# An encoder block on one core: modulation columns, output weights' sums and gate transposes placed earlier, pooling of one group placed later, and the end of each scan placed in the next head's scan

## The chip, the cores and the metric

The kernel runs on one core of a Trainium2 chip. The metric is the device time of one execution in microseconds (us); the kernel before takes 2042.19 us (median of three runs, 2037.84 to 2043.9).

The engines named below are TensorE (PE, with PEld for its weight loads), VectorE (DVE), ScalarE (ACT), GpSimd (POOL) and SyncE (SP). SP issues nearly all DMA transfers, in one queue.

## The reference, cut to what matters

One layer, 2048 tokens, model width 1024: modulation from `c`, a token mixer with two halves (a bidirectional mLSTM of 4 heads and a pooling of 4 channel groups), then a squared-ReLU MLP.

```
mod = silu(c) @ w_ada + b_ada              # 6 x 1024: sh1, sc1, gt1, sh2, sc2, gt2
h   = rmsnorm(x) * (1 + sc1) + sh1
q, k, v, o, gates, u = split(h @ w_in)     # 4 heads of 128; u: 4 groups of 128
hm  = scan_forward(q, k, v, gates) + scan_backward(...)     # in chunks of 128 tokens
y_a = sigmoid(o) * headnorm(hm) * g_head
y_b = ((mean of u over a window 2, 4, 8, 16) - u) @ w_pool * pool_scale
x   = x + gt1 * (concat(y_a, y_b) @ w_out)
h   = rmsnorm(x) * (1 + sc2) + sh2
x   = x + gt2 * (relu(h @ w_ff1)^2 @ w_ff2)
out = rmsnorm(x)
```

## The kernel before, in words

**Stages.** TensorE goes through the program in this order: a first part of the modulation (columns 0 to 15 of 48, each a 128x1024 piece of `w_ada`) and the projection of v and the gates (16 blocks of 128 tokens, `vg_mm` and `vg_out`); the pool stage (`for g in (3, 2, 1, 0)`, each with four blocks of 512 tokens); the q and k projection of head 0; four scans, each over 16 chunks, beside which the next head's projection (the last scan's: the o projection) is issued; then the output projection and the MLP, which the change does not touch.

**A projection block.** `col_mm(ci, b, w)` multiplies column group `ci` with token block `b`: 8 k-steps of three matmuls each, high weight by high activation (L404), high by low (L405) and low by high (L406). The split weights come from `col_weights(ci)`: a load of 512 KB into a buffer `wr`, a cast on ScalarE to `wh`, and on VectorE `wl = wr - wh` (L396). The pool stage uses column group 12+g for pool group g, so 15, 14, 13, 12, and then 4 for the q and k projection. The weights of the next one are asked for at block 1 of the group ahead of it.

**One group of the pool stage.** ScalarE copies each block's sum from PSUM into `u` (L440). When all four blocks are there, VectorE sums over the window by doubling (`s`, L447 and L451: one addition for window 2, four for window 16), mends the edges and subtracts `u` (L456); the result `yd` is stored. Then comes a fold: a piece of the output weights is loaded (`wor`), scaled on VectorE, multiplied with `w_pool` on TensorE (`wof`, two matmuls), copied and stored (`wod`). Then the modulation columns that `MODS[g]` lists are summed, each by `mod_col(j)`: a load of 512 KB (`ada`) and one multiply-and-sum on VectorE (L117).

**Gates.** `gate_rows` is a generator which the pool stage steps once per block. It transposes the gates (`gT`), makes log-sigmoids and running sums on VectorE and ScalarE, transposes the last elements (`gL`, L335), and later `gM`, `gC` and `gD`.

**Sums of the output weights.** `out_sums` makes the seven 512-wide combinations of `w_out * gt1` that the output projection wants: for each of four k two loads of 512 KB, two multiplications (L674), four subtractions (L682) and seven stores of 256 KB. It is stepped from the loop over the scans.

**Buffers.** `wr`, `ada`, `wor` and `os` (the tiles of `out_sums`) share three buffers (`raw`); evacuations share three (`evt`). Projection blocks share two PSUM buffers, folds two.

**Order.** The code's order is a starting point: a scheduler sets the order of each engine's instructions within what dependencies allow, save those that `keep_in_program_order` pins. Each engine then runs its instructions in the order that it was given.

Of the kernel before, what the change touches and what calls it, by code (L numbers as in the profile page):

```python
# [30 lines left out]
MODS = (range(16, 20), range(20, 28), range(28, 38), range(38, 48))  # L31
# [4 lines left out]
def block_kernel(ctx, tc, x, x_t, cb, w_ada, b_ada, g_mix, g_ffn, g_head, p_scale, w_col, w_vg,  # L36
# [96 lines left out]
    with tc.tile_pool(name="pv", bufs=1) as pv, tc.tile_pool(name="psV", bufs=2, space=PSUM) as psV:  # L133
# [156 lines left out]
        for b in range(NB):  # L290
            if b + 1 < NB:
                dg, xk = later_block(b + 1)
            for j in range(4):
# [6 lines left out]
                vg_out(4 * b + j)  # L300

# [8 lines left out]
    def gate_rows(pg):  # L310
# [22 lines left out]
        yield  # L333
        ps = tp("gL")
        pe.transpose(ps[0:1, 0:P], lasts[:, 0:1], ident)  # L335
# [16 lines left out]
        pe.transpose(ps[:, 0:1], rows[:, 3, :], ident[0:1, 0:1])  # L352
# [21 lines left out]
        yield  # L374
        ps = tp("gC")
        pe.transpose(ps[:, 0:P], v, ident)
# [36 lines left out]


    with tc.tile_pool(name="pu", bufs=2) as pu, tc.tile_pool(name="psU", bufs=2, space=PSUM) as psU:
# [7 lines left out]
        w = col_weights(15)  # L423
        for g in (3, 2, 1, 0):
            win = WIN[g]
            hw = win // 2
            u = pu.tile([P, T + 16], F32, tag="u", name=f"u{g}")
            gp.memset(u[:, 0:8], 0.0)
            gp.memset(u[:, T + 8:T + 16], 0.0)
            for b in range(NB):  # L430
# [10 lines left out]
                if b == 1:  # L441
                    wn = col_weights(11 + g if g else 4)
            w = wn

            s = pu.tile([P, T + 16], F32, tag="s", name=f"s{g}", bufs=1)
            n = T + 15
            ve.tensor_tensor(s[:, 0:n], u[:, 0:n], u[:, 1:n + 1], ALU.add)  # L447
            d = 2
            while d < win:
                n -= d  # L450
                ve.tensor_tensor(s[:, 0:n], s[:, 0:n], s[:, d:n + d], ALU.add)  # L451
                d *= 2
            s = s[:, 8 - hw:8 - hw + T]
            ve.tensor_tensor(s[:, 0:8], s[:, 0:8], edgec[:, 16 * g:16 * g + 8], ALU.mult)
            ve.tensor_tensor(s[:, T - 8:T], s[:, T - 8:T], edgec[:, 16 * g + 8:16 * g + 16], ALU.mult)
            ve.scalar_tensor_tensor(s, s, 1.0 / win, u[:, 8:8 + T], ALU.mult, ALU.subtract)  # L456
            for b in range(NB):
                dma(y_d[b][:, 4 + g, :], s[:, 512 * b:512 * b + 512])

            wr = raw(f"wor{g}")  # L460
            dma(wr, w_o[4 + g])
            ve.tensor_scalar(wr, wr, pscale[:, g:g + 1], None, ALU.mult)
            for n in range(2):
                ps = psU.tile([P, 512], F32, tag="y", name=f"wof{g}_{n}")
# [12 lines left out]
    with tc.tile_pool(name="ps_", bufs=2) as sp, tc.tile_pool(name="psS", bufs=1, space=PSUM) as psS:  # L477

        def qk_proj(h, C):
# [68 lines left out]
            for _ in p:  # L548
                yield

        def scan(h, Cb):
            X = {}

            def s0(c):
# [146 lines left out]
        for h in range(H):  # L701
# [6 lines left out]
            for _ in scan(h, Cb):  # L708
# [3 lines left out]
                if h > 0 and n % 4 == 0:  # L712
                    next(osum, None)
# [557 lines left out]
```

## Time and profile before

| | us |
|---|---|
| median of 3 runs (lowest, highest) | 2042.19 (2037.84, 2043.9) |
| profiled execution: device time, span in the trace | 2039.14, 2037.1 |
| TensorE busy | 1987.5 (98%) |
| VectorE busy | 1356.5 (67%) |
| ScalarE busy | 918.3 (45%) |
| GpSimd busy | 129.7 (6%) |
| data moved by DMA | 452.87 MB |

The device time of the profiled execution is 2 us above the span of its trace, and 3 us under the median of the timed runs. TensorE's granted clock is 0.997 of full speed over the execution. The stages of the trace, by TensorE's matmuls: the projection of v and the gates until 134.3 us, the pool stage until 239, q and k of head 0 until 290.6, the four scans from 290.6, 377.5, 459.7 and 534.5, and from 640 us the output projection and the MLP.

### The profile page before, as it was taken

To read this page: it belongs to the slowest core of one execution; us is meant where nothing else is said; L and a number is where in the kernel's file an instruction comes from. 1 tells how busy PE (TensorE), PEld (TensorE's weight loads), DVE (VectorE), ACT (ScalarE), POOL (GpSimd) and SP (SyncE) were. 2 spreads that over 40 slices of the span, in tenths; PEclk is the share of its full clock that TensorE was granted. 3 is DMA by queue.
4 is the path that set the end of the run, shared out by engine and by line. 5 is a ranking of instruction groups with operands and counts; after the bars stand their busy time and mean duration, and the time that the engine had idled before them with its cause. 6 is when DMAs were issued, how large, how long until landed. Compare 5 with 4: busy or idle time off the path is not lost.

```text
span 2037.1 us, 27780 instructions
## 1 busy us (share of the span) xinstructions
PE 1987.5 (98%) x9591; PEld 1658.5 (81%) x9591; DVE 1356.5 (67%) x2456; ACT 918.3 (45%) x1704; POOL 129.7 (6%) x353
## 2 busy tenths in 40 slices
PE   7999999989999999999999999999999999999998
PEld 6997777778887888888888888888888888888886
DVE  6638636676646777555666766666877667768876
ACT  4721223333335668755556655556324224324432
POOL 1100012222210111000000000000000000000011
PEclk9999999999999999999999999999999999999999
DMA  8736867787548799765666766766887657648553
GB/s 339 237 108 209 285 205 220 253 254 226 180 131 271 236 270 315 209 196 182 224 203 224 228 226 215 226 206 225 280 268 257 225 156 262 224 158 275 187 165 132
DMA packets 298574, 452.87 MB, mean 222 GB/s; under 512 B 23569, under 2 KB 163137, under 8 KB 298306
## 3 DMA queue, kind: packets, MB, share of 16 engines
q1 hardware_dynamic: 228546, 413.35, 62.3%
q10 hardware_dynamic: 69888, 37.76, 6.1%
q8 instruction: 75, 1.23, 0.2%
q14 instruction: 65, 0.53, 0.1%
HBM read 290.40 MB, written 160.62 MB: 221 GB/s over the span
## 4 chain that ended last, share of the span: by engine, by line
PE 84%; DMA 7%; DVE 4%; issue 1%; ACT 1%; POOL 1%; SPq 1%; POOLq 0%; DVEq 0%; ACTq 0%
PE c L405 4%; PE c L404 4%; PE c L406 4%; DMA ua<-uad 1%; DMA ada<-in_w_ada 1%; DVE ada L117 1%; DMA wotd<-os 1%; DMA rob<-wotd 1%; DMA vraw<-in_w_v 1%; PE f000x L845 1%; PE o11x L845 1%; PE o10x L845 1%; PE o13x L845 1%; PE o03x L845 1%; PE o12x L845 1%
## 5 line engine op out<-in xcount | busy, mean ns | idle before, releaser
L404 PE MATMUL c<-Hh,wh 128*128 128x512 f32 x512 | 211.0, 412 | 0.0
L405 PE MATMUL c<-Hl,wh 128*128 128x512 f32 x512 | 203.4, 397 | 0.0
L406 PE MATMUL c<-Hh,wl 128*128 128x512 f32 x512 | 202.8, 396 | 0.5 <-DVE wl L396 0.5
L406 PEld LDWEIGHTS c<-Hh,wl 128*128 128x128 f32 x512 | 96.6, 189 | 20.5 <-DVE wl L396 0.9
L404 PEld LDWEIGHTS c<-Hh,wh 128*128 128x128 f32 x512 | 97.0, 189 | 17.3 <-issue 1.0
L405 PEld LDWEIGHTS c<-Hl,wh 128*128 128x128 f32 x512 | 97.1, 190 | 16.8 <-issue 0.7
L117 DVE SCALAR_TENSOR_TENSOR ada<-ada,c_bc 128x1024 f32<-128x1024 f32 x48 | 58.1, 1221 | 22.4 <-DMA ada<-in_w_ada 22.3
L581 ACT ACTIVATE ua<-ua,vcol 128x128 f32<-128x128 f32 x64 | 25.7, 401 | 103.2 <-POOL ua L577 103.1
L780 ACT CAST wb<-rwb 128x1024 fp32r<-128x1024 f32 x56 | 58.7, 1051 | 26.0 <-DMA rwb<-twd 25.8
L961 POOL TENSOR_TENSOR g300ss<-g300ss 128x1 f32<-128x1 f32 x2 | 0.9, 451 | 1079.9 <-ACT g300j L957 1079.9
L783 DVE TENSOR_TENSOR wb<-rwb,wb 128x1024 fp32r<-128x1024 f32 x56 | 68.3, 1219 | 0.8 <-ACT wb L780 0.7
L622 ACT ACTIVATE jk<-hm 128x128 bf16<-128x128 f32 x64 | 19.6, 307 | 83.0 <-DVE hm L620 82.3
L586 DVE TENSOR_TENSOR ua<-ua,q 128x256 f32<-128x256 f32 x64 | 26.4, 425 | 37.5 <-DMA ua<-uad 26.8
L577 POOL TENSOR_SCALAR_AFFINE_SELECT ua<-ua 128x128 f32<-128x128 f32 x64 | 26.6, 416 | 270.7 <-DMA ua<-uad 135.4
L625 DVE TENSOR_TENSOR hm<-hm,hss 128x256 f32<-128x256 f32 x32 | 14.7, 458 | 38.9 <-POOL hss L129 38.9
L255 PE MATMUL vgp<-vgh,Hh 128*128 128x272 f32 x128 | 38.2, 301 | 2.3 <-ACT Hh L208 2.3
L440 ACT COPY u<-c 128x512 f32<-128x512 f32 x16 | 9.4, 585 | 63.7 <-PE c L406 59.4
L783 DVE TENSOR_TENSOR ob<-rob,ob 128x1024 fp32r<-128x1024 f32 x14 | 17.1, 1224 | 30.5 <-ACT ob L780 29.9
L256 PE MATMUL v2p<-v2h,Hh 128*128 128x256 f32 x128 | 36.2, 286 | 1.1 <-ACT v2h L236 1.1
L257 PE MATMUL vgp<-vgl,Hh 128*128 128x272 f32 x128 | 37.2, 292 | 0.0
L259 PE MATMUL vgp<-vgh,Hl 128*128 128x272 f32 x128 | 37.0, 294 | 0.0
L585 DVE TENSOR_TENSOR ua<-ua,S 128x256 f32<-128x256 f32 x64 | 26.5, 413 | 14.9 <-PE S L584 14.7
(4048 smaller groups left out, 6071.3 us busy)
## 6 DMA issues: line engine op xcount, KB each, us to landing
rwb<-twd SPq DMA_DIRECT2D x56, 512.0 KB, 6.1
ada<-in_w_ada SPq DMA_DIRECT2D x48, 512.0 KB, 5.2
ua<-uad SPq DMA_DIRECT2D x64, 256.0 KB, 4.1
j<-in_w SPq DMA_DIRECT2D x32, 512.0 KB, 5.4
twd<-t SPq DMA_DIRECT2D x64, 256.0 KB, 3.0
twd<-j SPq DMA_DIRECT2D x48, 256.0 KB, 2.8
wr<-in_w_col SPq DMA_DIRECT2D x16, 512.0 KB, 4.9
q<-qkd SPq DMA_DIRECT2D x32, 256.0 KB, 3.6
```

The lines of the kernel that those rows point to most:

```text
L117: ve.scalar_tensor_tensor(w, w, 1.0, c_bc, ALU.mult, ALU.mult, accum_out=mod[:, j:j + 1])
L255: pe.matmul(pa[:, :VG], hh, vgh[k], start=st, stop=False)
L256: pe.matmul(pb[:, :256], hh, v2h[k], start=st, stop=False)
L257: pe.matmul(pa[:, :VG], hh, vgl[k], start=False, stop=False)
L259: pe.matmul(pa[:, :VG], hl, vgh[k], start=False, stop=en)
L404: pe.matmul(ps, hh[:, k], Hh[b][:, k], start=k == 0, stop=False)
L405: pe.matmul(ps, hh[:, k], Hl[b][:, k], start=False, stop=False)
L406: pe.matmul(ps, hl[:, k], Hh[b][:, k], start=False, stop=k == KT - 1)
L577: gp.affine_select(W[:, 0], W[:, 0], pattern=[[1, P]], compare_op=ALU.is_ge, fill=NEG, base=0, channel_multiplier=-1)
L780: sc.copy(dst, src)
L783: ve.tensor_tensor(dst, src, asf(hi), ALU.subtract)
L845: pe.matmul(ps, a[:, k], b[:, k], start=start and k == 0 and n == 0, stop=k == 3 and n == 2, skip_group_check=not start)
```

## The change

1. Of the modulation's columns, 18 (16 to 33) are summed during blocks 8 to 13 of the projection of v and the gates (`VMODS`). The pool stage keeps 34 to 47, in another division (`MODS`).
2. `out_sums` becomes a function without steps that is called for k = 3, 2, 1, 0 at four places of the pool stage (`OSUMS`); `gt1` is made ahead of the stage. The scans no longer step it.
3. The gate transposes `gL`, `gM` and `gC` are pinned, and `gL` and `gC` come a block later.
4. The pooling of a group becomes the function `pooled`. That of group 3 is called, pinned, at the first block of group 2. Folds 3 and 2 stand behind group 3, folds 1 and 0 behind group 2 (`FOLDS`).
5. A scan's loop is one step shorter; its last pair of chunks is finished (`s3`, the transposes `hT`) at the start of the next head's scan.

```diff
-MODS = (range(16, 20), range(20, 28), range(28, 38), range(38, 48))
+VMODS = {i: range(16 + 3 * (i - 8), 19 + 3 * (i - 8)) for i in range(8, 14)}
+MODS = ((), range(44, 48), range(38, 44), range(34, 38))
+FOLDS = ((), (), (1, 0), (3, 2))
+OSUMS = {(2, 2): 3, (1, 0): 2, (1, 2): 1, (0, 0): 0}
...
                 vg_out(4 * b + j)
+                for n in VMODS.get(4 * b + j, ()):
+                    mod_col(n)
...
         yield
+        yield
         ps = tp("gL")
-        pe.transpose(ps[0:1, 0:P], lasts[:, 0:1], ident)
+        tc.keep_in_program_order(pe.transpose(ps[0:1, 0:P], lasts[:, 0:1], ident))
...
+    def out_sums(k, gt1):
+        rows = [raw(f"os{h}_{k}") for h in range(2)]
+        for h, src in enumerate((w_o[k], wo_d[k])):
+            dma(rows[h], src)
+        for h in range(2):
+            ve.tensor_tensor(rows[h], rows[h], gt1, ALU.mult)
+        b11, b12, b21, b22 = [r[:, 512 * n:512 * n + 512] for r in rows for n in range(2)]
+        for place, b in ((0, b11), (1, b21), (5, b22)):
+            dma(wot_d[place, :, k], b)
+        for place, dst, x_, y_ in ((3, b11, b12, b11), (4, b12, b22, b12), (2, b22, b22, b11),
+                                   (6, b21, b21, b22)):
+            ve.tensor_tensor(dst, x_, y_, ALU.subtract)
+            dma(wot_d[place, :, k], dst)
...
+        def pooled(g, u, pinned):
...
+            ins = ve.tensor_tensor(s[:, 0:n], u[:, 0:n], u[:, 1:n + 1], ALU.add)
+            if pinned:
+                tc.keep_in_program_order(ins)
...
                 if b == 1:
                     wn = col_weights(11 + g if g else 4)
+                if (g, b) in OSUMS:
+                    out_sums(OSUMS[g, b], gt1)
+                if (g, b) == (2, 0):
+                    pooled(3, u3, True)
             w = wn
...
+            if g == 3:
+                u3 = u
+            else:
+                pooled(g, u, False)
+            for f in FOLDS[g]:
+                wr = raw(f"wor{f}")
...
             for j in MODS[g]:
                 mod_col(j)
...
+            if ends:
+                ends.pop()()
-            for c in range(NT + 2):
+            for c in range(NT + 1):
...
+            if h + 1 < H:
+                ends.append(lambda: s3(NT - 1))
+            else:
+                s3(NT - 1)
...
-                if h > 0 and n % 4 == 0:
-                    next(osum, None)
```

What this does to the order of the engines' instructions is shown at three places. A number behind an underscore is that of the tile; `wl12` are the low weights of column group 12, `u1` and `s1` belong to pool group 1, and `os0_2` is the first of the two tiles of `out_sums` for k = 2.

VectorE between pool groups 1 and 0, of the kernel before:

```order
L396 TENSOR_TENSOR wl12_2066<-wr12_2063,wh12_2065 128x1024
L462 TENSOR_SCALAR wor1_2131<-wor1_2131,pscale_241 128x1024
L447 TENSOR_TENSOR s1_2121<-u1_2008 128x2063
L117 SCALAR_TENSOR_TENSOR ada20_2144,mod_90<-ada20_2144,c_bc_87 128x1024
L451 TENSOR_TENSOR s1_2121<-s1_2121 128x2061
```

and of the changed kernel (L454 and L460 are the additions of `pooled`, L429 and L435 the products and differences of `out_sums`, L405 is the subtraction for `wl`):

```order
L122 SCALAR_TENSOR_TENSOR ada43_2086,mod_90<-ada43_2086,c_bc_87 128x1024
L454 TENSOR_TENSOR s1_2237<-u1_2090 128x2063
L128 TENSOR_TENSOR mod_90<-mod_90,bada_200 128x1
L429 TENSOR_TENSOR os0_2_2119<-os0_2_2119,gt1_1660 128x1024
L429 TENSOR_TENSOR os1_2_2120<-os1_2_2120,gt1_1660 128x1024
L460 TENSOR_TENSOR s1_2237<-s1_2237 128x2061
L435 TENSOR_TENSOR os0_2_2119<-os0_2_2119 128x512
L405 TENSOR_TENSOR wl12_2165<-wr12_2162,wh12_2164 128x1024
```

`wl12` stood ahead of the first addition over `u1`; now it stands behind it and five more instructions, four of them long.

VectorE between pool group 0 and the q and k projection, before:

```order
L396 TENSOR_TENSOR wl4_2234<-wr4_2231,wh4_2233 128x1024
L462 TENSOR_SCALAR wor0_2298<-wor0_2298,pscale_241 128x1024
L117 SCALAR_TENSOR_TENSOR ada16_2311,mod_90<-ada16_2311,c_bc_87 128x1024
L447 TENSOR_TENSOR s0_2289<-u0_2176 128x2063
L123 TENSOR_TENSOR mod_90<-mod_90,bada_200 128x1
```

and of the changed kernel:

```order
L454 TENSOR_TENSOR s0_2393<-u0_2263 128x2063
L128 TENSOR_TENSOR mod_90<-mod_90,bada_200 128x1
L122 SCALAR_TENSOR_TENSOR ada47_2259,mod_90<-ada47_2259,c_bc_87 128x1024
L429 TENSOR_TENSOR os0_0_2292<-os0_0_2292,gt1_1660 128x1024
L128 TENSOR_TENSOR mod_90<-mod_90,bada_200 128x1
L429 TENSOR_TENSOR os1_0_2293<-os1_0_2293,gt1_1660 128x1024
L463 TENSOR_TENSOR s0_2393<-s0_2393,edgec_1644 128x8
L464 TENSOR_TENSOR s0_2393<-s0_2393,edgec_1644 128x8
L465 SCALAR_TENSOR_TENSOR s0_2393<-s0_2393,u0_2263 128x2048
L435 TENSOR_TENSOR os0_0_2292<-os0_0_2292 128x512
L405 TENSOR_TENSOR wl4_2338<-wr4_2335,wh4_2337 128x1024
```

`wl4`, too, stood ahead of the first addition over `u0`, and now stands ten instructions behind it. The load of `wr4` takes the buffer that `ada47` had, so it can be issued only when the sum over `ada47`, which now stands behind that addition, is done.

TensorE at the end of pool group 1, before:

```order
L406 MATMUL c13_3_2095<-Hh3_1052,wl13_1889 128x512
L404 MATMUL c12_0_2179<-Hh0_277,wh12_2065 128x512
L405 MATMUL c12_0_2179<-Hl0_278,wh12_2065 128x512
L406 MATMUL c12_0_2179<-Hh0_277,wl12_2066 128x512
L465 MATMUL wof1_0_2134<-wor1_2131,wpl_1570 128x512
L465 MATMUL wof1_1_2139<-wor1_2131,wpl_1570 128x512
L404 MATMUL c12_0_2179<-Hh0_277,wh12_2065 128x512
```

and of the changed kernel, where L413 to L415 are the three matmuls of a k-step:

```order
L415 MATMUL c13_3_2211<-Hh3_1052,wl13_1945 128x512
L413 MATMUL c12_0_2266<-Hh0_277,wh12_2164 128x512
L414 MATMUL c12_0_2266<-Hl0_278,wh12_2164 128x512
L413 MATMUL c12_1_2309<-Hh1_436,wh12_2164 128x512
L414 MATMUL c12_1_2309<-Hl1_437,wh12_2164 128x512
L415 MATMUL c12_0_2266<-Hh0_277,wl12_2165 128x512
```

Behind the last matmul of group 1, which `u1` needs, four matmuls stand that need no `wl12`; the fifth needs it. The fold that stood here is gone. The same four stand at the end of group 0, ahead of the first that needs `wl4`.

## Rows read from the trace of the kernel before

**Rows 1.** The page's first part, busy us (share of the span) and instructions; below it busy time of each engine by stretch of time (start:end, length; then the granted clock, DMA share, GB/s): the projection of v and the gates, the pool stage, q and k of head 0, the output projection and MLP.

```profile
PE 1987.5 (98%) x9591; PEld 1658.5 (81%) x9591; DVE 1356.5 (67%) x2456; ACT 918.3 (45%) x1704; POOL 129.7 (6%) x353
...
12.00:134.00 122.00, 113.50 (x853) 109.24 (x854) 72.42 (x158) 64.38 (x110) 11.01 (x41) 0.99 0.67 226
134.30:239.00 104.70, 99.17 (x416) 77.25 (x415) 78.64 (x155) 23.54 (x37) 0.62 (x9) 0.98 0.71 230
239.00:290.60 51.60, 49.39 (x238) 39.73 (x237) 22.96 (x45) 9.38 (x19) 3.18 (x8) 1.00 0.69 234
...
640.00:2037.00 1397.00, 1387.10 (x6175) 1146.72 (x6174) 971.49 (x1449) 695.59 (x1187) 38.69 (x96) 1.00 0.69 223
```

**Rows 2.** TensorE's waits, grouped by what it waited for: us in total, times, longest.

```profile
PE gL L335 <- issue: 4.1, 1, 4.1
...
PE kvb L508 <- DVE Cf L607: 2.7, 4, 1.2
PE hT L632 <- DVE hm L625: 2.7, 3, 1.0
...
PE wof L465 <- DVE wor L462: 0.9, 2, 0.8
```

**Rows 3.** The gates' chain in order of time, each fence line with start, length, engine, line, operation: on TensorE the last transpose `gT` and the first `gL`, on VectorE what stood between; last the stretch behind `gL` with its length, TensorE's busy time and granted clock.

```profile
145.51 0.27 PE L316 MATMUL gT<-ident,G 128*128 128x128 f32 x1
...
147.41 1.22 DVE L117 SCALAR_TENSOR_TENSOR ada<-ada,c_bc 128x1024 f32<-128x1024 f32 x1 [1.64 <-DMA ada<-in_w_ada]
...
148.56 0.35 DVE L317 TENSOR_SCALAR g_li<-gT,bgate 128x128 f32<-128x128 f32 x1
...
155.34 0.27 PE L335 MATMUL gL<-ident,g_last 128*1 128x128 f32 x1 [4.06 <-issue]
...
155.34:158.98 3.64, 3.60 (x10) 0.53 0.24 48
```

**Rows 4.** Groups of VectorE's instructions between 134 and 250 us, by form: busy us and mean ns of one, then idle time before them.

```profile
L117 DVE SCALAR_TENSOR_TENSOR ada<-ada,c_bc 128x1024 f32<-128x1024 f32 x32 | 38.9, 1221 | 16.8 <-DMA ada<-in_w_ada 16.7
L447 DVE TENSOR_TENSOR s<-u 128x2063 f32<-128x2063 f32 x4 | 9.2, 2303 | 0.2 <-ACT u L440 0.2
L456 DVE SCALAR_TENSOR_TENSOR s<-s,u 128x2048 f32<-128x2048 f32 x4 | 9.1, 2286 | 0.0
```

**Rows 5.** The ends of pool groups 1 and 0 in order of time: the last copy of `u1` on ScalarE, VectorE's `wl12`, `wor1` and first addition, TensorE's first matmul with `wl12`; then VectorE's `wl4`, the last copy of `u0`, and VectorE's first addition over it.

```profile
210.77 1.22 DVE L396 TENSOR_TENSOR wl<-wr,wh 128x1024 fp32r<-128x1024 f32 x1 [4.50 <-ACT wh L395]
211.15 0.59 ACT L440 COPY u<-c 128x512 f32<-128x512 f32 x1 [0.41 <-PE c L406]
211.91 0.75 DVE L462 TENSOR_SCALAR wor<-wor,pscale 128x1024 f32<-128x1024 f32 x1
212.05 0.50 PE L406 MATMUL c<-Hh,wl 128*128 128x512 f32 x1 [0.47 <-DVE wl L396]
212.58 2.30 DVE L447 TENSOR_TENSOR s<-u 128x2063 f32<-128x2063 f32 x1
214.79 1.22 DVE L117 SCALAR_TENSOR_TENSOR ada<-ada,c_bc 128x1024 f32<-128x1024 f32 x1
...
235.06 1.23 DVE L396 TENSOR_TENSOR wl<-wr,wh 128x1024 fp32r<-128x1024 f32 x1 [0.77 <-ACT wh L395]
235.93 0.58 ACT L440 COPY u<-c 128x512 f32<-128x512 f32 x1 [0.90 <-PE c L406]
239.41 2.31 DVE L447 TENSOR_TENSOR s<-u 128x2063 f32<-128x2063 f32 x1
```

**Rows 6.** The first three scans, columns as in rows 1; then the products (L674) and the differences (L682) of `out_sums` in the second scan alone, and the projection blocks' matmuls (tile c) in the first and the third.

```profile
290.64:377.48 86.84, 81.23 (x469) 67.96 (x468) 56.67 (x170) 28.09 (x86) 19.64 (x48) 1.00 0.74 231
377.48:459.65 82.17, 74.69 (x441) 62.87 (x439) 54.88 (x173) 26.29 (x83) 18.48 (x48) 1.00 0.79 250
459.65:534.50 74.85, 72.89 (x439) 63.24 (x440) 48.31 (x161) 26.31 (x83) 18.22 (x48) 1.00 0.67 205
...
377.48:459.65 82.17, 4.88 (x4) 1.00 0.79 250
377.48:459.65 82.17, 5.54 (x8) 1.00 0.79 250
...
290.64:377.48 86.84, 58.95 (x219) 38.55 (x218) 0.00 (x0) 5.44 (x10) 1.00 0.74 231
459.65:534.50 74.85, 51.84 (x191) 33.86 (x191) 0.00 (x0) 4.18 (x9) 1.00 0.67 205
```

**Rows 7.** DMA issues between 92 and 215 us (KB each, median us from issue to landing), and, from the lists by time, ScalarE's copy of the projection's block 13 and TensorE's first matmuls of the pool stage, of which L406 is the first to need `wl15`.

```profile
ada<-in_w_ada SPq DMA_DIRECT2D x23, 512.0 KB, 4.1
yd<-s SPq DMA_DIRECT2D x8, 256.0 KB, 3.1
wr<-in_w_col SPq DMA_DIRECT2D x2, 512.0 KB, 4.7
...
123.20 0.38 ACT L268 COPY vt<-vgp 128x256 f32<-128x256 f32 x1 [5.53 <-DVE G L266]
...
134.62 0.40 PE L405 MATMUL c<-Hl,wh 128*128 128x512 f32 x1
134.86 0.40 PE L406 MATMUL c<-Hh,wl 128*128 128x512 f32 x1
```

More of the change, by code (lines that the diff above doesn't have):

```diff
@@ L351, in gate_rows @@
         ps = tp("gM")
-        pe.transpose(ps[:, 0:1], rows[:, 3, :], ident[0:1, 0:1])
+        tc.keep_in_program_order(pe.transpose(ps[:, 0:1], rows[:, 3, :], ident[0:1, 0:1]))
         mp = gt("g_mp", 1)
@@ L374, in gate_rows @@
         yield
+        yield
         ps = tp("gC")
-        pe.transpose(ps[:, 0:P], v, ident)
+        tc.keep_in_program_order(pe.transpose(ps[:, 0:P], v, ident))
         pe.transpose(ps[:, P:2 * P], wk, ident)
@@ L442, in block_kernel @@
                     wn = col_weights(11 + g if g else 4)
+                if (g, b) in OSUMS:
+                    out_sums(OSUMS[g, b], gt1)
+                if (g, b) == (2, 0):
+                    pooled(3, u3, True)
             w = wn
[L445 to L464, printed above, removed]
-                pe.matmul(ps, wpl[:, g], wr[:, 512 * n:512 * n + 512], start=True, stop=True)
-                e = evt(f"woe{g}_{n}")[:, :512]
-                sc.copy(e, ps)
-                dma(wo_d[g][:, 512 * n:512 * n + 512], e)
+            if g == 3:
[4 more added lines that the diff above has]
+                wr = raw(f"wor{f}")
+                dma(wr, w_o[4 + f])
+                ve.tensor_scalar(wr, wr, pscale[:, f:f + 1], None, ALU.mult)
+                for n in range(2):
+                    ps = psU.tile([P, 512], F32, tag="y", name=f"wof{f}_{n}")
+                    pe.matmul(ps, wpl[:, f], wr[:, 512 * n:512 * n + 512], start=True, stop=True)
+                    e = evt(f"woe{f}_{n}")[:, :512]
+                    sc.copy(e, ps)
+                    dma(wo_d[f][:, 512 * n:512 * n + 512], e)
             for j in MODS[g]:
@@ L549, in qk_proj, with scan @@
                 yield
-        def scan(h, Cb):
+        def scan(h, Cb, ends):
             X = {}
@@ L697, in block_kernel @@
         dma(mod_d, me[0:48, 0:P])
-        gt1 = wp.tile([P, D], F32, tag="bc", name="gt1", bufs=1)
-        dma(gt1, mod_row(16))
-        osum = out_sums(gt1)
+        ends = []
         for h in range(H):
@@ L707, in block_kernel @@
             n = 0
-            for _ in scan(h, Cb):
+            for _ in scan(h, Cb, ends):
                 n += 1
```

42 lines of the change are left out of this document (22 added, 20 removed).

## The prediction, made before the changed kernel ran

> **What bounds the kernel now.** I read the busy times first: TensorE is busy for 1987.5 us of 2037.1, so an edit is worth what it does to TensorE's stops of some 50 us in all. By stretch, the output projection and MLP hold 9.9 us of them in 1397, the projection of v and the gates 8.5, the pool stage 5.5, q and k of head 0 2.2 [rows 1]; the MLP's instructions stand in the same order in both kernels, so what I work out lies ahead of 640 us. Next the waits: the largest in the pool stage is 4.1 us at `gL`; the scans' waits for VectorE (2.7 at `kvb`, 2.7 at `hT`) are short and many, and the folds cost 0.9 [rows 2]. Then the scans side by side: the first two take 86.84 and 82.17 us, the third, in which `out_sums` has no instruction, 74.85 [rows 6]. Last the list by time at the ends of pool groups 1 and 0: there VectorE has made `wl12` and `wl4` before it begins the long additions over `u1` and `u0` [rows 5].
>
> **The change part by part.**
>
> *Gate transposes.* TensorE stood 4.06 us at `gL`, and behind it the granted clock was 0.53 for 3.64 us, thus mostly the lower of its two levels, 1.2 GHz [rows 3]: about half of 3.64 was lost, 1.7. From the end of `gT` to `gL` the chain took 9.6 us (145.78 to 155.34), of which TensorE worked 5.5; in the changed kernel a whole block stands between in addition, 24 matmuls of 0.23, another 5.5, so it gets there 1.4 us after the chain's end. Both losses go: -5.8. The small waits at `wl12` (0.47 [rows 5]) and at the folds (0.9 [rows 2]) go from their places: -1.4.
>
> *Sums out of the scans.* The second and the third scan have the same work beside them but for `out_sums`: 82.17-74.85 = 7.3. The first carries 27 more projection matmuls (218 against 191 weight loads) of 0.227 us start to start: 86.84-6.1-74.85 = 5.9. Together -13.2. VectorE's own share is 10.4 us in the second scan (4.88+5.54), so the gain is not more than VectorE's time but part of it [rows 6]. Bounds: 8 (if only the stops of TensorE, 5.6+7.5, less the third's 2.0 each, go, 9.2, and a little is found again) and 16.
>
> *Eighteen columns in the projection of v and the gates.* Each costs VectorE 1.22 us [rows 4]: 22 us, three behind each of six blocks. Its copies out of PSUM for blocks 9 to 11 now stand behind two or three of the sums, so PSUM comes free later; of the up to 3.7 us that three sums take I take +1.0 (0 to 3), as a block of TensorE's work lies beside them. The load of `wr15` takes the buffer of `ada31`, whose own load stands behind the store of block 13, copied at 123.20 to 123.6. With 4.1 for a load, 1.2 for the sum and 4.7 for `wr15` it lands at 123.6+4.1+1.2+4.7 = 133.6 or, as two more loads lie beside it, 134.9; cast (1.05) and subtraction (1.22) end at 136 to 137.2, while TensorE wants it at 134.9 [rows 7]: +1.75 (0 to 4). That is +2.75.
>
> *Folds.* The second pair of the four `wof` behind `gL` waits for a PSUM buffer's copy: +0.5. Fold 1 waits for `wor1`, which stands on VectorE behind the whole pooling of group 3 (four additions and a subtraction of 2.3 each, with two products between): +1.8 (0 to 3).
>
> *`wl12` behind the pooling of group 1.* The last matmul of c13_3 releases the copy of `u1`, 0.6 us [rows 5]; VectorE then runs, start to start, the first addition 2.2 (212.58 to 214.79 [rows 5]), two products 1.15 each (they are as wide as L117, whose 1.22 overlaps the next by 0.08), the second addition 2.2, a difference 0.6 (5.54/8 = 0.69 less the overlap [rows 6]) and `wl12` 1.2: 9.2. TensorE has four matmuls of 0.23 for this time: it stops for 9.2-0.9 = **8.3**. The difference waits for the store of the block it overwrites; 3.1 for such a store [rows 7] lies beside the product and the addition, 3.35, so it adds nothing.
>
> *`wl4` behind the pooling of group 0.* Again 0.6 for the copy and 2.2 for the addition, 0.1, and the sum over `ada47` 1.15: 4.1 us after c12_3. Only then can the load of `wr4` be issued: 4.7, cast 1.05, subtraction 1.2, together 11.1. VectorE's own row (two products 2.3, edges 0.2, last pass 2.2, difference 0.6, `wl4` 1.2) ends at 10.6, so the load decides by a little. TensorE stops for 11.1-0.9 = **10.2** (9.7 to 11.5). Queued behind `wl4` is little that is due: c4_3 itself was 3.2 us after c12_3 before (fold 0 lay between), and is now the only work.
>
> *Clock.* After each of these two stops I expect what followed `gL`'s: 1.7 each, +3.4 (0 to 6.8 if it lasts twice as long).
>
> *The last chunks of a scan* move to the next scan's start in the code, but TensorE's order of the `hT` transposes stays what it was, save for a place of six matmuls in the last scan: 0 (a gain of 2.7 at most, the waits at `hT` [rows 2]).
>
> *Transfers.* The sums bring 28 stores and 8 loads into the pool stage (11 MB), and 18 loads (9.4 MB) leave it; its DMA share of 0.71 [rows 1] stays about the same. Counted at nothing, covered by that; if the cover fails, `wr4` is the one that shows it.
>
> **Sum.** -5.8-1.4-13.2 = -20.4; +2.75+0.5+1.8+8.3+10.2+3.4 = +26.95. Net +6.5: the profiled execution goes from 2039.1 to 2045.6, and as the median stood 3 us above it, the median from 2042.2 to 2048.7.
>
> **A rule weighed.** In the row of the gates VectorE took `g_li` only at 148.56, 2.8 us after `gT` (145.51+0.27), as the sum ahead of it waited for its load until 147.41 [rows 3]: a ready instruction did not pass a waiting one. By that row both stops stand in full. Were it otherwise, the two stops and their clock would fall away. The Trainium skill, page "PSUM — Partial Sum Buffer", section "Engine vs sequencer instructions", says that VectorE's queue is strictly first in, first out; the trace agrees, and by that rule the time is the sum above, 2048.7, without it 2026.8.
>
> **The rivals.**
> - *No stop at `wl12` and `wl4`*: VectorE takes them before the additions, as it did in the kernel before. Then -8.3-10.2-3.4: 2048.7-21.9 = 2026.8. For it: before, neither wait cost over half a us [rows 5]. Against it: the order now, and rows 3. It comes out faster by over 0.3% once 12.6 of these 21.9 us are gone.
> - *The scans gain all that the other stops hold too*: -20 in place of -13.2, as VectorE, with less to do, also ends the waits at `kvb` and `hT` that the third scan still has; 2042, within the bound. Against it: the third scan shows no gain beyond its 74.85.
> - *The clock stays down longer*, or falls after the smaller stops at blocks 9 to 11, `wl15` and fold 1 as well: +5, 2053.7. For it: a fall did follow the stop at `gL`; against: these stops are shorter than that one.
> - *The move does not do what it says for the scans*: their pace is set by something other than `out_sums` (the first two are slow for GpSimd or the load of `ua`), and -13.2 is 0: 2061.9. Against it: two scans with the same other work.
>
> **How the numbers follow.** A difference of 0.3% (6.1 us) is about what the measurement can tell from none, and the sum lies right at it. Chances: the sum as worked out 0.60 (2042 to 2055, half within 0.3% and half slower), longer low clock 0.14, scans unchanged 0.06, larger gain in the scans 0.10, no stops 0.10. So faster 0.12 (the last case, and 0.02 of the one before), same 0.38 (0.30 and 0.08), slower 0.50 (0.30, 0.14 and 0.06). The range 2036 to 2059 leaves out the case without stops (0.10) and most of the one with unchanged scans (0.05).
>
> **What would show it.** In the trace of the changed kernel: no wait at `gL` and full clock behind it; a stop of 8 to 9 us on TensorE between groups 1 and 0 and one of 10 to 11 between group 0 and c4_3, each released by `wl`, each followed by a lower granted clock; the pool stage with q and k of head 0 longer by 18 to 19 us, and the first two scans at 81 and 75. Wrong would be the prediction if `wl12` or `wl4` end within 3 us of the last matmul ahead of them, or if the first two scans stay above 85 and 80.

## The result, and the profile after

The changed kernel takes 2053.75 us (median of 7 runs, 2049.44 to 2061.03), the kernel before 2041.38 beside it: a ratio of 1.0064 (95% interval 1.0048 to 1.0079), so slower by 12 to 13 us. The profiled execution took 2054.34 us with a span of 2052.5, 15.4 more than the span of before; the terms below are counted against these 15.4.

Page of the changed kernel, busy times as in [rows 1]:

```profile
PE 1991.8 (97%) x9592; PEld 1662.6 (81%) x9592; DVE 1364.0 (66%) x2456; ACT 919.9 (45%) x1705; POOL 129.3 (6%) x353
```

TensorE's work is nearly the same: the lower clock adds to its busy time, the first two scans take 4 us off it (81.23 and 74.69 before [rows 6], 78.93 and 72.98 below), and 4 us more are left. What grew is its idle time. Its waits in the changed kernel, columns as in [rows 2]:

```profile
PE c L413 <- ACT wh L404: 21.4, 3, 10.1
...
PE wof L510 <- DVE wor L507: 2.7, 1, 2.7
PE hT L677 <- DVE hm L670: 2.6, 3, 0.9
...
PE c L415 <- DVE wl L405: 2.3, 1, 2.3
```

`gL` is gone from the list. In its place stand three stops at a new group's weights, 21.4 us in all, of which the first is at the start of the pool stage. By stretch: the projection of v and the gates, the pool stage up to c4_3, q and k of head 0, and three scans, columns as in [rows 1, 6]:

```profile
12.00:143.00 131.00, 112.99 (x857) 107.62 (x857) 93.47 (x212) 64.29 (x110) 12.52 (x47) 0.99 0.87 278
143.30:267.70 124.40, 104.27 (x411) 79.72 (x411) 83.03 (x135) 24.31 (x39) 0.28 (x4) 0.90 0.68 225
267.70:320.20 52.50, 52.49 (x240) 41.95 (x241) 17.86 (x34) 8.99 (x18) 2.11 (x8) 0.95 0.65 217
320.20:400.50 80.30, 78.93 (x469) 67.88 (x467) 49.10 (x158) 29.07 (x86) 18.58 (x48) 1.00 0.60 185
400.50:474.70 74.20, 72.98 (x441) 63.12 (x441) 48.70 (x161) 26.29 (x82) 18.29 (x48) 1.00 0.63 199
474.70:549.30 74.60, 73.00 (x441) 63.18 (x441) 49.00 (x161) 26.58 (x83) 18.82 (x48) 1.00 0.62 191
```

The pool stage starts 8.9 us later than before (143.3 against 134.4) and is 19.7 us longer (124.4 against 104.7), with a granted clock of 0.90 in it; with q and k of head 0 it is 20.7 longer (176.9 against 156.2), where the prediction expected 18 to 19. The first two scans are 80.3 and 74.2 us long, where they were 86.84 and 82.17 [rows 6]; the third is what it was.

The stop between pool groups 1 and 0, by time: ScalarE's last copy of `u1`, VectorE's row up to `wl12`, the cast of `wh12`, and TensorE:

```profile
224.10 0.39 PE L415 MATMUL c<-Hh,wl 128*128 128x512 f32 x1
224.53 0.58 ACT L491 COPY u<-c 128x512 f32<-128x512 f32 x1 [4.85 <-PE c L415]
225.20 2.31 DVE L454 TENSOR_TENSOR s<-u 128x2063 f32<-128x2063 f32 x1 [1.14 <-issue]
227.49 2.35 DVE L429 TENSOR_TENSOR os<-os,gt 128x1024 f32<-128x1024 f32 x2
229.76 2.30 DVE L460 TENSOR_TENSOR s<-s 128x2061 f32<-128x2061 f32 x1
232.58 1.22 DVE L405 TENSOR_TENSOR wl<-wr,wh 128x1024 fp32r<-128x1024 f32 x1
...
224.09 0.33 SPq L401 DMA_DIRECT2D wr<-in_w_col  x1
228.41 1.04 ACT L404 CAST wh<-wr 128x1024 fp32r<-128x1024 f32 x1 [3.31 <-DMA wr<-in_w_col]
...
229.51 0.80 PE L413 MATMUL c<-Hh,wh 128*128 128x512 f32 x1 [5.02 <-ACT wh L404]
233.85 0.80 PE L415 MATMUL c<-Hh,wl 128*128 128x512 f32 x1 [2.26 <-DVE wl L405]
```

VectorE ran exactly the row that the prediction worked out: from the copy's start to the end of `wl12` it took 9.3 us. But TensorE stopped first for `wh12` (5.02 us), the cast of a load that was issued only at 224.09, and then for `wl12` (2.26). Two things were late at once. The prediction expected `wl` to release both stops. The same at c4_3, where the load of `wr4` was issued behind the sum over `ada47`:

```profile
259.18 2.30 DVE L454 TENSOR_TENSOR s<-u 128x2063 f32<-128x2063 f32 x1
261.46 1.22 DVE L122 SCALAR_TENSOR_TENSOR ada<-ada,c_bc 128x1024 f32<-128x1024 f32 x1
262.72 0.33 SPq L401 DMA_DIRECT2D wr<-in_w_col  x1
266.57 1.04 ACT L404 CAST wh<-wr 128x1024 fp32r<-128x1024 f32 x1 [8.38 <-DMA wr<-in_w_col]
267.67 0.79 PE L413 MATMUL c<-Hh,wh 128*128 128x512 f32 x1 [10.10 <-ACT wh L404]
```

And the stretches of low clock in the pool stage, with TensorE's busy time in each (second number):

```profile
140.28:147.11 6.83, 3.79 (x8) 2.58 (x9) 4.34 (x9) 2.51 (x4) 0.00 (x0) 0.50 0.97 314
198.31:201.72 3.41, 3.41 (x7) 1.83 (x6) 1.47 (x1) 1.17 (x2) 0.00 (x0) 0.50 1.03 360
229.03:239.27 10.24, 7.49 (x17) 5.42 (x18) 10.14 (x11) 0.43 (x1) 0.00 (x0) 0.50 0.68 229
259.75:273.40 13.65, 5.73 (x13) 4.19 (x14) 11.54 (x15) 1.04 (x1) 0.00 (x0) 0.50 0.81 287
```

Each follows a stop of TensorE (6.30, 2.69, 7.28 and 10.10 us). 20.4 us of matmuls ran at 1.2 GHz in place of 2.4, by estimate a loss of half, 10.2 us; the kernel before had one such stretch in this stage [rows 3].

### The profile page after: what moved, and what is told of

Its sections match the earlier page's. It is cut to its first block, busy times and chain, and to the rows that moved or that the text cites. A ratio compares the mean times of both kernels' runs of the same rounds, so it can differ in the third digit from the quotient of the medians.

```text
span 2052.5 us, 27806 instructions
## 1 busy us (share of the span) xinstructions
PE 1991.8 (97%) x9592; PEld 1662.6 (81%) x9592; DVE 1364.0 (66%) x2456; ACT 919.9 (45%) x1705; POOL 129.3 (6%) x353
## 4 chain that ended last, share of the span: by engine, by line
PE 86%; DMA 6%; DVE 5%; ACT 1%; issue 1%; POOL 0%; SPq 0%; POOLq 0%; DVEq 0%; ACTq 0%
PE c L413 4%; PE c L414 4%; PE c L415 4%; DMA ada<-in_w_ada 2%; DVE ada L122 1%; DMA ua<-uad 1%; DVE xk L224 1%; PE S L629 1%; PE kvf L647 1%; PE n L643 1%; PE n L640 1%; DMA vraw<-in_w_v 1%; PE n L642 1%; PE n L645 1%; DVE Hl L214 1%
## 5 line engine op out<-in xcount | busy, mean ns | idle before, releaser
L413 PE MATMUL c<-Hh,wh 128*128 128x512 f32 x512 | 214.9, 420 | 21.4 <-ACT wh L404 21.4
L415 PE MATMUL c<-Hh,wl 128*128 128x512 f32 x512 | 204.1, 399 | 2.3 <-DVE wl L405 2.3
L413 PEld LDWEIGHTS c<-Hh,wh 128*128 128x128 f32 x512 | 98.7, 193 | 39.3 <-ACT wh L404 22.6
L415 PEld LDWEIGHTS c<-Hh,wl 128*128 128x128 f32 x512 | 98.0, 191 | 24.9 <-DVE wl L405 4.3
```

Source lines behind the costliest of these rows:

```text
L413: pe.matmul(ps, hh[:, k], Hh[b][:, k], start=k == 0, stop=False)
L415: pe.matmul(ps, hl[:, k], Hh[b][:, k], start=False, stop=k == KT - 1)
```

## The experiments

The medians of the kernel before beside which these ran lie between 2039.39 and 2043.49 us; each ratio is against the runs of its own batch, and comes from all of them, not from the two medians.

**Gate transposes alone.** The kernel before with part 3 of the change:

```diff
         yield
+        yield
         ps = tp("gL")
-        pe.transpose(ps[0:1, 0:P], lasts[:, 0:1], ident)
+        tc.keep_in_program_order(pe.transpose(ps[0:1, 0:P], lasts[:, 0:1], ident))
...
```

> The kernel before with part 3 alone (gate transposes pinned, gL and gC a block later). My account: the 4.06 us stop at gL and the lower clock behind it (1.7 us lost) both go, nothing takes their place: about 2041.4 - 5.8 = 2035.6. Rival: the later gL only moves the wait to gC or to the decay factors that the q and k projection needs, so the time stays within 2 us of 2041.4 and a stop of some 4 us stands at another line.

Measured: 2038.38 us, ratio 1.0004 (0.9992 to 1.0017). The wait at `gL` is gone, and a wait of about the same size stands at the next transpose, `gM`:

```profile
PE gM L353 <- DVE g_rows L350: 4.8, 1, 4.8
...
163.14 2.29 DVE L449 TENSOR_TENSOR s<-u 128x2063 f32<-128x2063 f32 x1
166.05 2.27 DVE L453 TENSOR_TENSOR s<-s 128x2061 f32<-128x2061 f32 x1
168.25 0.17 DVE L349 COPY g_rows<-g_rows 1x60 f32<-1x60 f32 x1
```

The little copies that `gM` needs stand on VectorE behind group 3's first two additions, which come free at that time. The rival holds: alone, this part only moves the wait. In the changed kernel part 4 defers group 3's pooling to group 2, and there neither wait appears. That the two parts work together there is likely, but no run has them without the others.

**Columns alone.** The kernel before with part 1 (`VMODS` and the new `MODS`).

> The kernel before with part 1 alone (18 columns beside the projection of v and the gates, the rest in the pool stage). If these loads and sums by themselves make the pool stage start late, it starts at 142 to 144 us as in the changed kernel (134.4 before) with a stop of 5 to 7 us at the weights wh15, and the time is 2041.4 + 8.9 for the later start + 1 to 2 for the clock behind the stop, less at most 1 in the pool stage: 2050 to 2052. If the late start came from other parts (gt1's path, the two folds' loads), it starts before 138 us and the time is under 2046.

Measured: 2038.36 us, ratio 0.9997 (0.9985 to 1.001). The stretch up to the pool stage, and the first scan:

```profile
12.00:141.40 129.40, 113.98 (x856) 109.08 (x856) 94.03 (x212) 64.47 (x110) 11.89 (x46) 0.99 0.86 281
290.60:376.90 86.30, 81.19 (x468) 67.90 (x467) 56.35 (x170) 27.90 (x86) 19.95 (x48) 1.00 0.71 232
```

The pool stage starts 7.1 us late (141.5 against 134.4), with a stop of 4.2 us at `wh15`, close to what was expected. But all of it is given back: the first scan starts at 290.6 us, as before. From the start of the pool stage to the first scan TensorE is idle for 1.6 us in place of 7.7, and its wait at `gL` falls from 4.1 to 1.3 us though part 3 is not in this kernel. Where I took a late start for a loss, the part moves idle time from one stage to the other.

**The order on VectorE alone.** The changed kernel with pins:

```diff
-        ve.tensor_tensor(hl, r, asf(hh), ALU.subtract)
+        ins = ve.tensor_tensor(hl, r, asf(hh), ALU.subtract)
+        if pin:
+            tc.keep_in_program_order(ins)
...
-                    wn = col_weights(11 + g if g else 4)
+                    wn = col_weights(11 + g if g else 4, True)
...
-                pooled(g, u, False)
+                pooled(g, u, True)
```

> The changed kernel with the subtractions that make wl13, wl12 and wl4 pinned, and all four poolings pinned behind them, so that on VectorE wl12 and wl4 stand ahead of the first additions over u1 and u0 again; loads keep their buffers. If the order on VectorE makes the two stops, both fall under 1.5 us: 17.4 us of stops and some 6 of lower clock go, about 2030. If the loads that share three buffers make them (wr12 landed 3.9 us after the last matmul of group 1 in the changed kernel, and wl12 now stands behind the whole of one out_sums call), a stop of 7 to 10 us stays at group 0's start and 3 to 8 at c4_3, and the time is 2046 to 2055.

Measured: 2062.45 us, ratio 1.0115 (1.01 to 1.013). With `wl12` and `wl4` ahead of the additions, the stop ahead of group 0 is twice as long (14.3 us, in two pieces), the one at c4_3 about the same (9.2 us), and a third of 3.6 us comes at `wl13`. ScalarE and TensorE ahead of group 0:

```profile
238.87 1.04 ACT L404 CAST wh<-wr 128x1024 fp32r<-128x1024 f32 x1 [10.90 <-DMA wr<-in_w_col]
239.97 0.80 PE L415 MATMUL c<-Hh,wh 128*128 128x512 f32 x1 [12.62 <-ACT wh L404]
243.71 0.79 PE L417 MATMUL c<-Hh,wl 128*128 128x512 f32 x1 [1.67 <-DVE wl L405]
```

My theory of the order, by itself, falls: the load of `wr12` comes late whatever VectorE's order. That a held buffer is why, the run with one buffer more shows.

**The sums out of the pool stage.** The changed kernel with `out_sums` taken out of it and stepped, pinned, in the last scan:

```diff
-                if (g, b) in OSUMS:
-                    out_sums(OSUMS[g, b], gt1)
...
+                if h == H - 1 and n > 2:
+                    next(osum, None)
```

> The changed kernel with out_sums taken out of the pool stage and stepped in the last scan, pinned there. VectorE then has wl12 and wl4 ahead of the additions over u1 and u0, and no loads of out_sums lie in the pool stage. Both theories of the two stops (order, loads) expect them under 1.5 us; the later start of the pool stage (8.9 us) stays. The last scan, where TensorE was busy 105.4 of 105.5 us and VectorE 48.7, takes the 21 us of VectorE's work: my account says it hides there (under 2 us longer): about 2053.7 - 17.4 - 6 - 1 = 2029. Rival: it costs in the last scan what it cost in the first two, 13 us: 2042.

Measured: 2046.01 us, ratio 1.0036 (1.0022 to 1.0049). The pool stage of this kernel, and its last scan up to the output projection; below it the same stretch of the kernel before:

```profile
143.10:247.00 103.90, 103.83 (x431) 81.38 (x432) 66.07 (x116) 24.75 (x39) 0.28 (x4) 0.97 0.53 182
521.60:655.00 133.40, 118.13 (x589) 98.45 (x587) 71.58 (x178) 42.91 (x99) 16.73 (x40) 0.95 0.75 241
```

```profile
534.50:646.00 111.50, 110.78 (x586) 93.88 (x584) 53.80 (x153) 42.05 (x99) 15.81 (x40) 1.00 0.57 184
```

TensorE is never idle in the pool stage (0.07 of 103.9 us), the first scan starts at 291.6 us (290.6 before, 320.2 in the changed kernel), and the last starts at 521.6, 13 us earlier than before. So the sums in the pool stage, with the row of `gt1` that they need there, cost the changed kernel 28.6 us, which is more than all of its loss: what they cost there and what the first two scans gain without them, 14.5 us, differ by 14.1, nearly the whole 15.4. But the last scan grows by 22 us: the sums cost there more than the 13 us that they cost in the first two, with waits of 7.4 us at `hT` for VectorE. My "hides there" was wrong: VectorE, busy for half of that scan before, was not free for work that stands in its queue ahead of the scan's steps.

**The sums on GpSimd.** The kernel before, products and differences on GpSimd:

```diff
-                    ve.tensor_tensor(rows[h], rows[h], gt1, ALU.mult)
+                    gp.tensor_tensor(rows[h], rows[h], gt1, ALU.mult)
...
-                    ve.tensor_tensor(dst, x_, y_, ALU.subtract)
+                    gp.tensor_tensor(dst, x_, y_, ALU.subtract)
```

> The kernel before with the products and differences of out_sums on GpSimd in place of VectorE, still stepped from the scans. If the sums cost the first two scans their 13 us through VectorE's time and its waits for their loads and stores, those scans fall to some 80 and 75 us: 2039.4 - 13 = 2026 if GpSimd has room (it was busy 19.6 us of 86.8 there). If GpSimd's share, the masks on ua that every chunk waits for, is held up behind the sums' waits, the scans stay as long or grow: 2039 to 2050.

Measured: 2052.04 us, ratio 1.0069 (1.0054 to 1.0084). The first two scans grow to 93.0 and 87.8 us, the third stays at 74.5. In these two scans GpSimd waits 21.9 us for the sums' transfers, and ScalarE waits 65.8 us for the masks on `ua` that GpSimd makes (58.3 before). That fits the rival, with a time a little above its range; the share of the masks in the loss was not taken apart.

**Weights first.** The changed kernel with the next group's weights asked for at block 0, ahead of the columns and the sums, and pinned:

```diff
-                if b == 1:
-                    wn = col_weights(11 + g if g else 4)
+                if b == 0:
+                    wn = col_weights(11 + g if g else 4, True)
+                    for j in MODS[g + 1] if g < 3 else ():
+                        mod_col(j)
...
-            for j in MODS[g]:
-                mod_col(j)
```

> The changed kernel with the next group's weights asked for at block 0, ahead of the previous group's modulation columns and of out_sums (so wr12 and wr4 get a buffer before these loads), with wl13, wl12, wl4 and all poolings pinned. Order on VectorE and order of the loads are then both mended. My account now: the two stops (17.4 us) come from the two together, either alone suffices to keep them; so both fall to under 2 us each and the time to about 2053 - 15 - 5 = 2033. If what stops TensorE is simply that VectorE has too much to do in this stage (busy near 90 us of 115), stops of the same sum come up elsewhere (folds, gates, PSUM copies) and the time stays above 2045.

Measured: 2065.03 us, ratio 1.0126 (1.011 to 1.0141). The stop at the start of group 0 is gone. The one at c4_3 is longer, 6.3 us for `wh4` and 10.3 for `wl4`, and a new one stands at `kvb`:

```profile
PE kvb L555 <- DMA va<-vd: 11.7, 1, 11.7
PE c L417 <- DVE wl L405: 10.3, 1, 10.3
...
247.44 1.23 DVE L431 TENSOR_TENSOR os<-os,gt 128x1024 f32<-128x1024 f32 x1 [5.39 <-DMA os<-wod]
```

VectorE sits waiting at a product for the sums' load while `wl4` stands behind it, and behind the product come the two long additions of group 1's pooling, still ahead of `wl4`. The time is what the second theory said, above 2045; but VectorE was waiting here, not too busy. The same with the sums on GpSimd:

> As the kernel with the weights first, and the products and differences of out_sums on GpSimd, which had nothing to do in the pool stage (0.62 us busy). Order, loads and VectorE's time are all relieved: no stop over 2 us behind the start of the pool stage, scans at 80 and 75, about 2030. If GpSimd is so slow at these (a product of 128x1024 over 4 us) that their buffers come free late, the loads of wr4 and of the last columns wait for them and a stop of 5 us or more stays at c4_3: 2038 or more.

Measured: 2076.19 us, ratio 1.0181 (1.0164 to 1.0198), with stops of 8.5 us at fold 1, 13.6 at the weights and 15.5 at `kvb`. A product took GpSimd 4.0 us here (median), and from the first load of a pair of `os` tiles to the issue of its last store it took 18 to 36 us, in the changed kernel 14 to 27.

**The ends of the scans alone.** The kernel before with part 5.

> The kernel before with part 5 alone (a scan's last pair of chunks finished in the next head's scan). My account: TensorE's order is the same but for the last scan, so within 3 us of 2039.4, waits at hT as before (2.7 us in all). Rival: the waits at hT at the heads' ends go, 2.7 us, and the next scan starts earlier: 2036 or less.

Measured: 2037.61 us, ratio 1.0001 (0.9985 to 1.0016). The waits at `hT` at three heads' ends are 0.92, 0.91 and 0.86 us, as before: the part does nothing.

**One buffer more.** The changed kernel, one edit and room for it. This kernel leaves out the row `gt1`: the products take the row of `c` in its place, so it computes something else, and only its time says anything:

```diff
-        r = raw(f"wr{ci}").rearrange("p (k n) -> p k n", k=KT)
+        r = raw(f"wr{ci}") if own is None else own.tile([P, D], F32, tag="wrp", name=f"wr{ci}", bufs=1)
+        r = r.rearrange("p (k n) -> p k n", k=KT)
...
-                    wn = col_weights(11 + g if g else 4)
+                    wn = col_weights(11 + g if g else 4, pu)
...
-        gt1 = pu.tile([P, D], F32, name="gt1", bufs=1)
-        dma(gt1, mod_row(16))
+        gt1 = c_bc
```

> The changed kernel with one buffer more: the raw weights wr13, wr12 and wr4 get a buffer of their own and no longer share the three with ada, wor and os. To make room, the tile of gt1 is left out and the products of out_sums take another vector of the same shape, so this is for its time alone. Nothing is pinned beyond the changed kernel's pins; VectorE's order follows the loads, with wl12 and wl4 ahead of the additions. Theory of the three buffers (in the changed kernel each os tile holds one for some 18 us, from its load to its last store, so the 8 os, 14 ada, 4 wor and the weights fill three buffers for the whole stage): both stops go (under 2 us each), the stop at the start of the pool stage stays, and the time is 2053 - 17.4 - 5 = about 2031. Theory of VectorE's load (too much work in the stage, whatever the buffers): stops of at least 10 us in all stay between 143 us and the first scan, and the time is above 2042.

Measured: 2036.69 us beside 2043.49, ratio 0.9967 (0.9956 to 0.9979). The pool stage up to the last copy of `u0`, and the first two scans:

```profile
143.30:244.00 100.70, 99.86 (x417) 77.95 (x418) 72.22 (x119) 24.18 (x39) 0.28 (x4) 0.98 0.75 241
299.40:380.30 80.90, 79.27 (x468) 67.76 (x466) 49.06 (x157) 29.15 (x86) 18.25 (x48) 1.00 0.60 184
380.30:455.70 75.40, 73.34 (x440) 63.16 (x440) 48.44 (x160) 26.31 (x82) 18.87 (x48) 1.00 0.66 196
```

Both stops are gone with VectorE's whole work still in the stage: up to the first scan it is busy for 100.2 us here, 100.9 in the changed kernel, and 101.6 in the kernel before, so the change did not put more work there. That the three buffers are what makes `wr12` and `wr4` late is thus shown; VectorE's order follows from it, as nothing was pinned here and `wl12` and `wl4` stand ahead of the additions again. Against the changed kernel's 1.0064 the time is 0.97% less, some 20 us, where this theory gave 22.4.

**The sums spread.** The kernel before, each step of the sums pinned where the code has it, over heads 1 to 3:

> The kernel before with the products and differences of out_sums pinned where the code steps them, one every fourth step of heads 1 to 3, so that they spread over 302 to 600 us in place of 302 to 446 us. If the scans lose their 13 us through VectorE's waits for the sums' loads and stores (each step now has some 6 us for its transfer), most of the 13 us comes back: 2029 to 2033. If VectorE's time itself is what delays the scan's steps, the loss spreads over three heads and stays: 2038 to 2042. If the tiles hold their buffers so long that the weights of the next projection come late, stops at the projection appear: over 2042.

Measured: 2054.78 us, ratio 1.0073 (1.005 to 1.0095). The second and the third scan:

```profile
373.10:458.00 84.90, 75.75 (x440) 64.33 (x440) 54.15 (x169) 25.92 (x82) 18.39 (x48) 0.98 0.71 217
458.00:540.20 82.20, 71.66 (x416) 59.79 (x417) 54.13 (x171) 24.95 (x80) 18.48 (x48) 0.97 0.75 226
```

Each scan that holds the sums pays: the second and the third take 10.1 and 7.4 us more than a scan without them (74.85 [rows 6]), the fourth 10 more than before. VectorE never waits for a load or store of the sums here (6.8 us before), so the waits for these are not the price: VectorE's 20.8 us of them still delay `hm`, `Cf` and `Cb` ahead of TensorE (7.0 us of waits at `hT` alone). The time lies above the 2042 of the second case, and not for the reason of the third: TensorE waits only 1.9 us for a projection's weights. One rival is left: VectorE waits longer for the loads of `ua` (45.8 us, before 26.8), so the sums' transfers may have their part.

**The buffer, whole computation.** As above with `gt1` kept; room comes from the pooling's weights and the gates' row:

```diff
-        rows = pg.tile([1, 4, P], F32, name="g_rows")
+        rows = gcols[0:1]
...
-        wpl = pu.tile([P, 4, P], F32, name="wpl", bufs=1)
-        dma(wpl, w_pool)
...
+                wpl = pu.tile([P, P], F32, tag="wpl", name=f"wpl{f}", bufs=2)
+                dma(wpl, w_pool[:, f])
```

> The changed kernel with the buffer of its own for wr13, wr12 and wr4, and the whole computation: room for it comes from the pooling's weights (two small tiles in place of one large) and from the gates' row, which shares a tile with the gates' columns. The run without gt1's tile was 0.33% faster than the kernel before; theory of the buffers expects the same here, 2034 to 2039 with no stop over 2 us between 144 us and the first scan. If the missing tile of gt1 (its path by way of DRAM, its wait) helped that run, this one is 3 us or more slower than 2037.

Measured: 2047.13 us, ratio 1.0027 (1.0017 to 1.0038).

```profile
PE kvb L552 <- DMA va<-vd: 6.4, 1, 6.4
PE c L412 <- ACT wh L403: 6.2, 1, 6.2
PE wof L509 <- DVE wor L506: 4.1, 1, 4.1
```

No stop at `wl12` or `wl4` here either (the one at `wh` is that at the start of the pool stage), and 0.37% less than the changed kernel's 1.0064, but the time of the run without `gt1`'s tile doesn't come back: fold 1 waits 4.1 us, and behind c4_3 the load of `va` stands in SP's queue behind the sums' late stores. From 142.6 us to the first scan at 310.8 TensorE is idle for 13.5 us. By the bounds set for the run without `gt1` (stops of at least 10 us in all, a time above 2042) this would speak for the theory of VectorE's load. VectorE's work is the same, though (100.8 us), and the two longest waits are for a transfer and for `wor1`. So the buffer ends the two stops, but not the loss: of the 28.6 us that the sums cost in this stage, 19.2 are still there. Then with 12 columns beside the projection of v and the gates:

> As the kernel with its own buffer and the whole computation, but with 12 columns instead of 18 beside the projection of v and the gates (blocks 8 to 11), the other 6 in the pool stage. The load of wr15 then no longer waits for the buffer of a late column: the stop of 7 us at the start of the pool stage falls to under 2 us and the pool stage starts near 136. If the ring of three has room for six more columns in the pool stage, the gain stays: 2030 or 2031. If not, the first scan starts near 299 us again and the time is 2036 to 2038.

Measured: 2046.29 us, ratio 1.0021 (1.0012 to 1.003). The stop at the start of the pool stage is gone, as expected, and one of 16.7 us stands at `kvb`. The list names the store `kwd<-kf` for it; in SP's queue that store and the load of `va` both stand behind the sums' last four stores, until 272.1 us. The first scan starts at 309.2, and the time is above both cases (at most 2038). That the ring of three had no room for six more columns is likely; the rows show only what stood in SP's queue. No version with the whole computation beats the kernel before.

## Why the prediction was right, and where its sizes were off

Forecast was slower at the edge of what can be measured (2048.7, range 2036 to 2059); it is slower by twice as much. Against the profiled executions the sum missed by 8.7 us (2045.6, measured 2054.34); the medians lie only 5 apart because the 3 us by which the median stood above the profiled execution, and which the forecast added, were -0.6 in the changed kernel. By the steps of the sum:

| step | predicted | measured |
|---|---|---|
| `gL` and the clock behind it | -5.8 | -5.8 |
| small waits at `wl12` and folds | -1.4 | -1.4 |
| sums out of the scans | -13.2 | -14.5 (86.84 to 80.3, 82.17 to 74.2) |
| 18 columns: start of the pool stage | +2.75 | +8.9 |
| folds | +2.3 | +2.7 |
| stop at `wl12` | +8.3 | +7.3 |
| stop at `wl4` | +10.2 | +10.1 |
| clock behind the stops | +3.4 | +10.2 |
| the rest up to the first scan, clock apart | 0 | -2.4 |
| sum | +6.5 | +15.1 (spans: +15.4) |

The rest is TensorE's idle time in q and k of head 0, 2.2 us before [rows 1] and none after.

**Right in sign and size:** the gain in the scans, the two long stops and their place, that part 5 brings nothing, and that VectorE's waiting instruction isn't passed by a ready one (the row at 123.05 below). The rival without stops is out. (The terms at `wl12` add up to 9.1, not 9.2; nothing hangs on it.)

**The step on the gates** came out at its number, in part by luck. The prediction gave -5.8 to part 3. Alone, part 3 gains nothing, as the wait moves to `gM`; and part 1 alone already takes most of the wait at `gL`. Which part earns the 5.8 us in the changed kernel is not shown.

**The step on the columns** was mis-sized by 6.2 us. Its chain had the load of `wr15` issued at 123.6+4.1+1.2 = 128.9 us; it was issued at 136.8. A part of this is "4.1 for a load", the median of another stretch: between 93 and 143 us the columns' loads took 5.0, and up to 7.4, with the stores of `vd` between them (4.8 where they took 3.0 before). Even 7.4 explains only 3.3 of the 7.9 us; the rest is that the chain goes round several times:

```profile
ada<-in_w_ada SPq DMA_DIRECT2D x16, 512.0 KB, 5.0
vd<-vt SPq DMA_DIRECT2D x7, 258.0 KB, 4.8
...
123.05 1.23 DVE L122 SCALAR_TENSOR_TENSOR ada<-ada,c_bc 128x1024 f32<-128x1024 f32 x1 [4.75 <-DMA ada<-in_w_ada]
124.20 0.18 DVE L271 COPY G<-vgp 128x16 f32<-128x16 f32 x1
```

A sum waiting for its load held the copies of the next block behind it on VectorE, the store that follows those copies held SP's queue, and the next loads stood behind that store. I had three of these in a line once; they go round block by block. And the term was no loss by itself: alone, the columns cost nothing, since the pool stage gave their delay back.

**The step on the clock** was mis-sized by 6.8 us: I priced each fall by the one behind `gL`, where the stop was 4.1 us. Behind the two long stops the low level held for 5.7 and 9.8 us after work began again, which cost by estimate 6.6 us in place of 3.4, and it also followed the two stops that I had left out (at `wh15` and at fold 1), another 3.6. This was the rival of the lower clock, and it came true. That its 2053.7 is nearly the median measured is luck: it left out the columns' 6.2 us, and smaller errors and the 3 us above went the other way.

**The cause of the two stops** was named by half. VectorE's order is a consequence; the three buffers shared by loads of weights, columns and sums are what both the order and the late loads follow from. The prediction used this for `wr4` and `wr15`, not for `wr12`, so that its 8.3 for a measured 7.3 is right with half of its cause. The experiments with more room and with the sums taken out show it; the one with the order alone mended shows that the order isn't enough. For the whole loss the two stops are not the only cause: with room and the whole computation 0.27 of the 0.64% stayed, with stops at fold 1 and at `kvb` in their place.

What stays open is why the run with all of `gt1` is slower than the one without its tile by 10 to 12 us. All of it lies ahead of the first scan, which starts at 310.8 us in the one and at 299.4 in the other. Its own path through DRAM, the two more small loads, and the other order that the scheduler then chose changed together, and I did not take them apart. Nor is it settled how much of the sums' price in the scans is VectorE's time and how much their transfers ahead of the loads of `ua`.

## What to carry to other kernels

When work is moved into a stage whose loads turn over in a few shared buffers, count how long each tile holds its buffer (here a pair of `os` tiles 17 us, from its first load's issue at 221.4 to its last store's at 238.0), not only what its instructions cost; a full ring delays the next weights and, through the scheduler, the order of other engines. Price a transfer by a stretch as crowded as the new place will be, and a stop by its clock too. A part that gains or loses time at one place is worth running alone: three of the five parts here, alone, changed nothing that can be measured. With the columns and with the gates the next step gave back or took what the first had; the ends of the scans moved nothing.

## What the runs showed of the hardware that I had not expected

The lower clock level begins within a long stop and stays when work has begun again: in the changed kernel 3.8 us of work behind a stop of 6.3, 5.7 us behind one of 10.1, and 7.5 us where a second stop of 2.3 followed a first of 5.0. The four stretches together cost, by estimate, as much as the longest stop. How long it stays does not follow from the stop's length: it was 6.2 us behind a stop of 7.0 (the sums out of the pool stage), 4.2 behind 13.6 (weights first, sums on GpSimd) and 5.4 behind 16.7 (twelve columns). And it also came behind a stop of 2.7, at fold 1 (3.4 us).

GpSimd's product of 128x1024 took 2.39 us (median) in the scans and 4.03 in the pool stage, where VectorE ran its long passes over `u` and `s` beside most of them:

```profile
L674 POOL TENSOR_TENSOR os<-os,gt x8: 2359/2386/2400, 303.4 to 447.9; 128x1024 f32<-128x1024 f32 x8
```

```profile
L431 POOL TENSOR_TENSOR os<-os,gt x8: 2337/4027/4532, 184.6 to 288.0; 128x1024 f32<-128x1024 f32 x8
```

VectorE needs 1.22 for the same [rows 6]. That the two disturb each other is what the pool stage itself suggests: there the product at 262.1 us, with VectorE idle, took 2.34 us, and ten differences of 128x512 beside an idle VectorE 1.26 to 1.29, where four beside its long instructions took 3.2 to 3.4. Not every one was slow, though: two products beside VectorE's last pass took 2.4. Which pairs of instructions disturb each other was not taken apart.
